# Second norm of the feed-forward blocks: its steps written tile by tile into one slot, between the steps of the tile before the last, with the samples' operands staged

## The chip, the cores and the metric

The kernel runs on one core of a Trainium2 chip. Five engines work from queues of their own: PE (matmuls and transposes, results into PSUM), ACT (activations, copies, square roots), DVE (elementwise work), POOL (elementwise work on SBUF), and SP, which issues DMAs. Each engine works its queue off in the order of the program. The metric is the device time of one execution in microseconds (us). A time is the median of several runs; one further execution carries the hardware profiler.

## The reference

One layer of a decoder runs on a prompt of 2048 rows and on 8 samples of 4 rows (32 rows), with the same weights; the width is 1024. What the change touches is the end of the layer:

```python
y = concat(attention_heads, sgu_heads) @ w_out      # 1024 x 1024
x = x + y                                           # residual
z = rmsnorm(x, g2)                                  # the second norm: x / sqrt(mean(x*x) + 1e-6) * g2
h = silu(z @ w_gate) * (z @ w_up)                   # hidden width 2816
x = x + h @ w_down
out = rmsnorm(x, g_final)
```

## The kernel before

**Blocks.** The prompt is 16 row tiles of 128 rows. The attention comes first; then the out projection and the feed-forward part run in three blocks, `blocks = [Block(0,6), Block(6,12), Block(12,16)]`: block 0 and block 1 have six tiles, block 2 has four and also the 32 sample rows, which it works as a fifth, short tile (number 4 of that block, taken first: the order there is 4, 0, 1, 2, 3). A block goes through these stages:

1. The open units: columns 0 to 511 of the out projection of each tile (`open_part`), added to the residual (`open_end`).
2. The second phase, called so below: columns 512 to 1023 of each tile (`out_part`, L1360 to L1372), which is 24 matmuls with 512 columns for a tile (8 slices, three matmuls each, since a number is kept as a high and a low part), in two halves of 12. Then comes `out_end` (L1374 to L1382, DVE), which adds them to the residual `acc`, and the second norm.
3. The product of the gate and up weights by the normed rows, made from seven products (q0 to q6) in place of eight, over f = 0 to 21 (slices of the hidden width); for f = 0 in two units: unit 1 does the first four tiles (the first two in block 2), unit 2 the other two. Later f do all tiles at once. Between them stand the down products (L1654).

**The second norm of a tile** (L1400 to L1465) goes as follows. `norm2_a`: ACT squares a row and sums it (L1404, or L1411 where no half was squared early). `rms_b`: DVE L1386 and L1387, then ACT's square root (L1388). `norm2_b`: four short steps on DVE (`newton`, L142 to L146), then ACT writes the scaled row into a `pair` tile (L1420). `norm2_c`: eight transposes on PE into the two PSUM banks `ps_t` (L1433), then the operands of the seven products. ACT copies a quarter (L1449) and writes the first high part (L1450), DVE makes sums and differences (L1451, L1453, L1456, L1457) and low parts (L1452, L1458), `split_sb` (L132 to L138) writes the high part of a sum on ACT (L135) and its low part on POOL (L138), ACT writes two high parts from PSUM (L1455). Only when L1458 has read the second bank of `ps_t` may the next tile's transposes go into it. There are two such banks in all. High and low parts go into `xh2` and `xl2` (`B.X`).

**The samples** have four times fewer columns to spread: each of their seven operands is written by `split_sb(at_(hi), at_(lo_), x, eng_lo=dve)` (L1465) into columns 64 to 71 of every tile's place: 7 instructions on ACT and 7 on DVE behind one copy and four sums, from `norm2_c(B, n - 1, B.xns)` at the end of `next_block`, that is after the last tile's `out_part`.

**What sets the order.** Each engine's order is that in which the program is written, and `later(n, fn, ..., ahead=...)` and `tick()` (L1271 to L1282) write it: a `tick` stands ahead of every half of an `out_part`, ahead of every product q, and ahead of every down unit; `later(n, fn)` puts `fn` at the n-th tick from now, and with `ahead=True` in front of the others of that tick. `first_operands` (L1784) lays the weights' operands for f = 0 over ticks 1 to 9 of the second phase: `high` (ACT, L1520) and `low_half` (POOL or DVE, L1524). `next_block` lays `half1_split` (the split of `w_out`'s second half, L135 on ACT and L138 on POOL) at ticks 8, 11, 14 and 17. In before, `norm2_c` of a tile falls between the two halves of a later tile's `out_part`.

**Products.** `product` (L1571) does 12 matmuls into one of four banks `ps_m` and evicts them (L1590 to L1616): q0 on ACT, q1, q3 and q4 on DVE, q2 and q5 with a silu on ACT. The bank of q3 stays in use until the second eviction of q4 (L1602, `c22 = c21 + s1`).

Of the kernel before, what the change touches and what calls it, by code (L numbers as in the profile page):

```python
# [10 lines left out]
F32 = mybir.dt.float32  # L11
# [54 lines left out]
def hymba_step(ctx: ExitStack, tc: tile.TileContext, A: dict, O: dict):  # L66
# [99 lines left out]
    def zn_tile():  # L166
        return rp.tile([P, 512], F32, name="zn", tag="zn", bufs=3)
# [1089 lines left out]
    def square_tile():  # L1257
        return pair_tile(F32).rearrange("p a b -> p (a b)")
# [25 lines left out]
    class Block:  # L1284
        def __init__(self, b0, b1):
            self.b0, self.nt = b0, b1 - b0
            self.last = b1 == NT
            self.rows = [P] * self.nt + ([SR] if self.last else [])

            self.w = 64 + (SR // 2 // self.nt if self.last else 0)  # L1290
            self.acc, self.wo, self.cat, self.late, self.h, self.open, self.s1 = {}, {}, {}, {}, {}, {}, {}

        def place(self):
            self.X = []
# [95 lines left out]
    def rms_c(s1, n):  # L1390
        v, r = s1[:n, 1:2], s1[:n, 2:3]
        newton(r, v)
        return r
# [6 lines left out]
    def norm2_a(B, i, put_off):  # L1400
        n = B.rows[i]
        if i in B.s1:
            s1 = B.s1.pop(i)
            act.activation(B.X[0][:, i, 0:512], B.acc[i][:, 512:1024], AF.Square, accum_out=s1[:, 3:4])  # L1404
            later(1, rms_b, s1, n, s1[:, 3:4])
        else:
            s1 = fl.tile([P, 4], F32, name="s1", tag="s1", bufs=6)

            if n != P:
                B.xns = fc.tile([P, D], F32, name="xns", tag="acc5")  # L1410
            act.activation(B.X[0][:, i, 0:D] if n == P else B.xns[:n], B.acc[i][:n], AF.Square, accum_out=s1[:n, 0:1])  # L1411
            later(1, rms_b, s1, n)

        later(2, norm2_b, B, i, s1, put_off, ahead=True)

    def norm2_b(B, i, s1, put_off):
        n = B.rows[i]
        r = rms_c(s1, n)
        xn = square_tile() if n == P else B.xns
        act.activation(xn[:n], B.acc[i][:n], AF.Copy, scale=r)  # L1420
        if n == P:
            later(2 + put_off, norm2_c, B, i, xn)

    def norm2_c(B, i, xn):

        n = B.rows[i]
        hi, lo_ = B.ops
        pts = []
        for kk in range(2):
            pt = ps_t()  # L1430
            for k in range(4):
                c0 = (kk * 4 + k) * P
                pe.transpose(pt[:, k * P:k * P + n], xn[:n, c0:c0 + P], ident[:n, :n])  # L1433
            pts.append(pt.rearrange("p (k t) -> p k t", k=4)[:, :, 0:n].rearrange("p k (z t) -> p z k t", z=2))
        (b11, b12), (b21, b22) = ((p_[:, 0], p_[:, 1]) for p_ in pts)
        sums = [zn_tile()[:, 0:2 * 4 * (n // 2)].rearrange("p (j k t) -> p j k t", j=2, k=4) for _ in range(2)]
        (t1, t2), (t3, t4) = ((s_[:, 0], s_[:, 1]) for s_ in sums)

        def sums_of():

            act.activation(t4, b12, AF.Copy)
            dve.tensor_sub(t1, t4, b11)
            dve.tensor_sub(t3, b22, t4)
            dve.tensor_sub(t2, b22, t1)
            dve.tensor_sub(t4, b21, t2)

        if n == P:
            at_ = lambda x, j0, j1: x[:, i, j0:j1, :, 0:64]
            act.activation(t4, b12, AF.Copy)  # L1449
            act.activation(at_(hi, 0, 1)[:, 0], b11, AF.Copy)  # L1450
            dve.tensor_sub(t1, t4, b11)  # L1451
            dve.tensor_sub(at_(lo_, 0, 1)[:, 0], b11, at_(hi, 0, 1)[:, 0].bitcast(F32))  # L1452
            dve.tensor_sub(t2, b22, t1)  # L1453
            split_sb(at_(hi, 3, 5), at_(lo_, 3, 5), sums[0])
            act.activation(at_(hi, 1, 3), pts[1], AF.Copy)  # L1455
            dve.tensor_sub(t3, b22, t4)  # L1456
            dve.tensor_sub(t4, b21, t2)  # L1457
            dve.tensor_sub(at_(lo_, 1, 3), pts[1], at_(hi, 1, 3).bitcast(F32))  # L1458
            split_sb(at_(hi, 5, 7), at_(lo_, 5, 7), sums[1])
        else:  # L1460
            sums_of()
            for j, x in enumerate((b11, b21, b22, t1, t2, t3, t4)):
                at_ = lambda y: y[:, :, j, :, 64:].rearrange("p i k c -> p k i c")
                x = x.rearrange("p k (i c) -> p k i c", i=B.nt)
                split_sb(at_(hi), at_(lo_), x, eng_lo=dve)  # L1465

# [262 lines left out]
    def open_end(B, i):  # L1729
        out_end(B, i, 0, B.open.pop(i))  # L1730
# [64 lines left out]
            tick()  # L1795
            open_part(B, i, range(c * 4, c * 4 + 4), c == 0, c == 1)

    def second_unit(B, i):
        ps = ps_o()
        for c in range(2):  # L1800
            tick()
            out_part(B, i, 1, range(c * 4, c * 4 + 4), ps, c == 0, c == 1)
        return ps

    def second_end(B, i, ps, put_off=0):
        out_end(B, i, 1, ps)
        norm2_a(B, i, put_off)

    def first_block(B):

        m1, m2 = acc_place(2), acc_place(4)
        load_cat(B, 1, 0, KD, m1)
        merge_load(h, 2)
        merge_load(h, 3)
        load_cat(B, 2, 0, KD, m2)
        B.place()
        load_cat(B, 3, 0, KD)
        load_cat(B, 0, KD - 1, KD)
        load_acc(B, 1)
# [21 lines left out]
        for i in range(6):  # L1841
            ps = second_unit(B, i)
            if i in (1, 2):
                load_acc(B, 2 * i)
                load_acc(B, 2 * i + 1)
            if i > 1:
                open_end(B, i)
            second_end(B, i, ps, i == 5)

    def first_end(B, i):  # L1850
        open_end(B, i)
# [3 lines left out]
    def next_block(B, downs, finals):  # L1855

        n = len(B.rows)
        order = [n - 1] * B.last + list(range(B.nt))
        B.banks = {i: y for y, i in enumerate(order)}
        B.place()  # L1860
        tiles = [i for i in order if B.rows[i] == P]
        skip = n - len(tiles)
        for j, i in enumerate(tiles):
            if j < 3:
                load_cat(B, i, 0, KD)
            else:
                later(2 * j - 5, load_cat, B, i, 0, KD)
            later(3 + 2 * (j + skip), split_cat, B, i)
        half1_load(*range(4))
        later(3, half1_load, *range(4, KD))  # L1870
        for s in (6, 7):
            later(s - 5, split_wo, B, 0, s, lambda s: op_tile())
        for y, fn in enumerate(finals):
            later(2 + 2 * y, fn)
        for y, i in enumerate(order):
            later(12 + 2 * y, first_end, B, i)
        for y in range(4):
            later(8 + 3 * y, half1_split, B, 2 * y, 2 * y + 1)
            later(10 + 3 * y, sources, B, 0, *((2 * y, 2 * y + 1) if y < 3 else (6,)))
        for fn in downs:  # L1880
            fn()
        for i in order:
            open_unit(B, i)
        first_operands(B)
        for i in order:
            second_end(B, i, second_unit(B, i), i == order[-1])
        if B.last:
            norm2_c(B, n - 1, B.xns)

    for bi, B in enumerate(blocks):  # L1890
        if bi == 0:
# [190 lines left out]
```

## Time and profile before

| | us |
|---|---|
| runs (3) | 2655.63, 2662.3, 2672.53 |
| median | 2662.3 |
| profiled execution | 2665.7 |
| its span | 2663.9 |

The profiled execution lies 3.4 us above the median and within the spread of the runs. All numbers from the trace belong to it. A row of the timeline reads: start in us from the span's start, duration in us, engine, line, operation, output<-inputs, shapes, and how many records it stands for; a bracket at the end gives the idle time of that engine before it and what released it. Durations of matmuls overlap; what a matmul costs is the distance from its start to the next one's. A row of the windows view gives a stretch, its length, PE's busy time with the number of its matmuls, the clock that PE was granted (1.00 is full), the share of DMA and GB/s. A row of a groups view gives the count, the busy time and the mean ns of one, then the engine's idle time ahead of the group and what ended it.

The second phases and unit 1 after them stand in these places: block 0 from 995.97 to 1063.92, block 1 from 1616.80 to 1678.56, block 2 from 2207.24 to 2260.36, where unit 2 starts.

### The profile page before, as it was taken

The page shows a single profiled execution, that of the slowest core. Times are in us where ns is not written, and L with a number is a line of the kernel's source. Part 1 is how long each engine was busy: PE and PEld are TensorE (multiplying, and loading weights), DVE is VectorE, ACT ScalarE, POOL GpSimd, SP SyncE. Part 2 cuts the span into 40 slices and gives each one's busy share as a digit, 9 for nine tenths or more (in the row PEclk, how much of TensorE's full clock was granted, in tenths as well). Part 3 has the DMA queues.
Part 4 walks back from the last instruction along what each step waited for, and adds up shares of the span by engine and source line. Part 5 has one row for each costly group of instructions (what it writes and reads, how often), then busy time and mean ns, then how long its engine had stood idle before and what let it go on. Part 6 is the DMA issues. An engine that isn't in the chain of part 4 may idle for free. (4 is left out here: it accounts for less than half of the span.)

```text
span 2663.9 us, 38923 instructions
## 1 busy us (share of the span) xinstructions
PE 2509.5 (94%) x13587; PEld 2217.7 (83%) x13587; DVE 1419.8 (53%) x2828; ACT 1224.6 (46%) x2570; POOL 1367.8 (51%) x1040
## 2 busy tenths in 40 slices
PE   7999899998999888999999999999999998999997
PEld 6777687677888766898999987899999987999996
DVE  3358785435888845434444464444444465344445
ACT  5414344445887735554454544432333335433333
POOL 1035653132666654776776743554454533666663
PEclk9999999998999998999999999999999999899998
DMA  7765844587688573455463664455463643555553
GB/s 241 220 204 161 277 141 137 171 260 223 186 239 239 138 215 108 147 186 166 161 195 124 194 182 138 165 173 181 150 206 127 221 153 100 186 203 197 198 201 114
DMA packets 313811, 481.06 MB, mean 181 GB/s; under 512 B 25843, under 2 KB 178852, under 8 KB 307728
## 3 DMA queue, kind: packets, MB, share of 16 engines
q1 hardware_dynamic: 301052, 455.89, 53.3%
q10 hardware_dynamic: 12564, 22.68, 3.4%
q8 instruction: 108, 1.77, 0.3%
q14 instruction: 87, 0.71, 0.1%
HBM read 382.76 MB, written 165.84 MB: 206 GB/s over the span
## 5 line engine op out<-in xcount | busy, mean ns | idle before, releaser
L1524 POOL TENSOR_TENSOR op<-fr,op 128x512 fp32r<-128x512 f32 x385 | 488.9, 1297 | 311.1 <-ACT op L1520 291.3
L1581 PE MATMUL ps_m<-xh,op 128*128 128x384 f32 (+4 forms) x1932 | 623.6, 323 | 6.7 <-DVE zn L1602 3.3
L1583 PE MATMUL ps_m<-xh,op 128*128 128x384 f32 (+4 forms) x1932 | 622.0, 322 | 1.7 <-POOL op L1524 1.7
L1582 PE MATMUL ps_m<-xl,op 128*128 128x384 f32 (+4 forms) x1932 | 622.1, 322 | 0.9 <-DVE xl L1452 0.9
L1654 PE MATMUL ps_o<-dw,hw 128*128 128x512 f32 x2040 | 485.9, 393 | 11.8 <-DVE acc L1656 11.8
L1654 PEld LDWEIGHTS ps_o<-dw,hw 128*128 128x128 f32 x2040 | 380.5, 188 | 95.1 <-DVE acc L1656 18.9
L1581 PEld LDWEIGHTS ps_m<-xh,op 128*128 128x128 f32 x1932 | 371.8, 192 | 11.9 <-ACT xh L135 3.7
L1582 PEld LDWEIGHTS ps_m<-xl,op 128*128 128x128 f32 x1932 | 372.2, 193 | 5.4 <-DVE xl L1452 1.3
L1583 PEld LDWEIGHTS ps_m<-xh,op 128*128 128x128 f32 x1932 | 371.7, 192 | 2.1 <-POOL op L1524 2.1
L1656 DVE TENSOR_TENSOR acc<-acc,ps_o 128x512 f32<-128x512 f32 (+1 forms) x362 | 247.0, 687 | 215.0 <-PE ps_o L1654 215.0
L1621 ACT ACTIVATE ps_t<-zn 128x384 f32<-128x384 f32 (+1 forms) x126 | 58.3, 462 | 479.6 <-DVE zn L1604 372.2
L1520 ACT ACTIVATE op<-fr 128x512 fp32r<-128x512 f32 x396 | 235.5, 622 | 24.2 <-DMA fr<-ab_d 14.0
L138 POOL TENSOR_TENSOR dw<-fd,dw 128x1024 fp32r<-128x1024 f32 x66 | 158.7, 2404 | 123.5 <-ACT dw L135 123.1
L318 PE MATMUL ps_s<-wh,xh 128*128 128x512 f32 x480 | 196.8, 410 | 6.5 <-ACT xh L135 6.5
L319 PE MATMUL ps_s<-wl,xh 128*128 128x512 f32 x480 | 191.7, 399 | 4.6 <-DVE wl L226 4.4
L320 PE MATMUL ps_s<-wh,xl 128*128 128x512 f32 x480 | 191.3, 398 | 0.0
L1524 POOL TENSOR_TENSOR op<-pair,op 128x512 fp32r<-128x512 f32 x63 | 81.5, 1301 | 119.1 <-ACT op L1520 119.1
L1631 ACT ACTIVATE hw<-ps_t 128x384 fp32r<-128x384 f32 (+1 forms) x126 | 56.1, 453 | 176.6 <-DVE ps_t L1627 175.7
L318 PEld LDWEIGHTS ps_s<-wh,xh 128*128 128x128 f32 x480 | 92.4, 192 | 35.9 <-issue 8.2
L319 PEld LDWEIGHTS ps_s<-wl,xh 128*128 128x128 f32 x480 | 92.6, 193 | 23.5 <-DVE wl L226 6.3
L320 PEld LDWEIGHTS ps_s<-wh,xl 128*128 128x128 f32 x480 | 92.2, 192 | 20.7 <-POOL xl L138 0.4
L611 POOL TENSOR_TENSOR vl<-kv,vh 100x512 fp32r<-100x512 f32 (+1 forms) x32 | 46.0, 1440 | 109.9 <-ACT vh L605 35.5
(470 smaller groups left out, 4816.7 us busy)
## 6 DMA issues: line engine op xcount, KB each, us to landing
fr<-ab_d SPq DMA_DIRECT2D x308, 256.0 KB
fd<-in_w_down_dram SPq DMA_DIRECT2D x66, 512.0 KB
out_ks_dram<-in_cache_k_dram SPq DMA_DIRECT2D x56, 512.0 KB
out_vs_dram<-in_cache_v_dram SPq DMA_DIRECT2D x56, 512.0 KB
ab_d<-fr SPq DMA_DIRECT2D x88, 256.0 KB
raw<-in_w_in_dram SPq DMA_DIRECT2D x72, 256.0 KB
qk_d<-pair SPq DMA_DIRECT2D x64, 256.0 KB
ab_d<-pair SPq DMA_DIRECT2D x63, 256.0 KB
```

The lines of the kernel that those rows point to most:

```text
L138: (eng_lo or pool).tensor_sub(lo, src, hi.bitcast(F32))
L318: pe.matmul(o[j], xh[:, k, :], wh, start=(k == 0), stop=False)
L319: pe.matmul(o[j], xh[:, k, :], wl, start=False, stop=False)
L320: pe.matmul(o[j], xl[:, k, :], wh, start=False, stop=(k == KD - 1))
L1520: act.activation(ops[f, j][0], ab[f][j], AF.Copy)
L1524: (pool if f or j in POOL_LOW else dve).tensor_sub(lo_, ab[f][j], hi.bitcast(F32))
L1581: pe.matmul(out, wh[:, ks], xh[:, :, k], start=(k == 0), stop=False)
L1582: pe.matmul(out, wh[:, ks], xl[:, :, k], start=False, stop=False)
L1583: pe.matmul(out, wl[:, ks], xh[:, :, k], start=False, stop=(k == 3))
L1621: act.activation(g, c, AF.Silu)
L1654: pe.matmul(ps[0:nr], l_, r_[:, cs], start=(z == 0 and y == 0), stop=(z == FC - 1 and y == len(pairs) - 1))
L1656: dve.tensor_add(B.acc[i][0:nr, cs], B.acc[i][0:nr, cs], ps[0:nr])
```

## The change

The steps of the second norm are no longer put off one by one with `later`, but are written in one function, `norm2_slot(B, k, order)`, which stands ahead of the `out_part` of the k-th tile. It does the second norm's sum, root and scale for the tile whose `out_part` has just ended (`order[k-1]`), woven with the transposes and operands of the tile before that (`order[k-2]`). Two more slots follow the last tile: one ahead of product q0 of unit 1, one ahead of q4 (`later(1, ...)` and `later(5, ...)`, `ahead=True`).

- **Norm.** The instructions of `norm2_a` to `norm2_c` are the same; only their order is new. The operands are in four steps: `first` (PE's transposes, ACT's copy and first high part, DVE's five differences in a row), `second` (a split on ACT and POOL, ACT's two high parts from PSUM), `third` (the other split) and `last` (DVE's low part from PSUM). Between them stand the square, the short steps and the scale of the other tile.
- **Samples.** The short tile's operands are written like any other tile's, into a staged tile `xst` in SBUF, and `place_staged` copies them into columns 64 and on of every tile's place with one instruction on ACT and one on DVE, ahead of the slot that follows the last `out_part` (k = n). With the sums, the samples' operands took 8 instructions on ACT and 11 on DVE; now they take 6 on ACT and 7 on DVE, the two copies among them, and 2 on POOL.
- **Splits of `w_out`.** In block 2 `half1_split` moves from ticks 8, 11, 14, 17 to 8, 10, 12, 14.
- The loads of `acc` of tiles 2 to 5 in block 0 stay at the same place (`more_acc`).

No matmul, transpose or DMA is added or removed.

```diff
+    def norm2_scale(B, i, r):
+        ...
+        act.activation(B.xn[i][:n], B.acc[i][:n], AF.Copy, scale=r)
...
+    class Operands:
+        def __init__(self, B, i):
+            ...
+                    pe.transpose(pt[:, k * P:k * P + n], xn[:n, c0:c0 + P], ident[:n, :n])
+            ...
+            if n == P:
+                self.to = [x[:, i, :, :, 0:64] for x in B.ops]
+            else:
+                t_ = fc.tile([P, D], F32R, name="xst", tag="acc5")
+                B.staged = [t_[:, z * 512:z * 512 + 28 * SR // 2] for z in range(2)]
+                self.to = [x.rearrange("p (j k c) -> p j k c", j=7, k=4) for x in B.staged]
+        def first(self):
+            ...
+            act.activation(t4, b12, AF.Copy)
+            act.activation(hi[:, 0], b11, AF.Copy)
+            dve.tensor_sub(t1, t4, b11)
+            dve.tensor_sub(lo_[:, 0], b11, hi[:, 0].bitcast(F32))
+            dve.tensor_sub(t2, b22, t1)
+            dve.tensor_sub(t3, b22, t4)
+            dve.tensor_sub(t4, b21, t2)
+        def second(self):
+            split_sb(hi[:, 3:5], lo_[:, 3:5], self.sums[0])
+            act.activation(hi[:, 1:3], self.pts[1], AF.Copy)
+        def third(self):
+            split_sb(hi[:, 5:7], lo_[:, 5:7], self.sums[1])
+        def last(self):
+            dve.tensor_sub(lo_[:, 1:3], self.pts[1], hi[:, 1:3].bitcast(F32))
+    def place_staged(B):
+        for z, eng in enumerate((act, dve)):
+            src = B.staged[z].rearrange("p (m i c) -> p i m c", m=28, i=B.nt)
+            dst = B.X[z].rearrange("p i (m w) -> p i m w", m=28)[:, :, :, 64:]
+            ...
+    def norm2_slot(B, k, order):
+        n = len(order)
+        cur = order[k - 1] if 1 <= k <= n else None
+        x = None
+        if k == n and B.last:
+            place_staged(B)
+        if cur is not None:
+            if cur in B.open:
+                open_end(B, cur)
+            out_end(B, cur, 1, B.half1.pop(cur))
+        if 2 <= k:
+            x = Operands(B, order[k - 2])
+            x.first()
+        if cur is not None:
+            s1, more = norm2_square(B, cur, zn_tile() if k == n and B.last else None)
+        if x:
+            x.second()
+        if cur is not None:
+            rms_b(s1, B.rows[cur], more)
+            r = rms_c(s1, B.rows[cur])
+        if x:
+            x.third()
+        if cur is not None:
+            norm2_scale(B, cur, r)
+        if x:
+            x.last()
...
+    def second_phase(B, order, after=None):
+        for k, i in enumerate(order):
+            norm2_slot(B, k, order)
+            B.half1[i] = ps = ps_o()
+            for c in range(2):
+                tick()
+                out_part(B, i, 1, range(c * 4, c * 4 + 4), ps, c == 0, c == 1)
+            if after:
+                after(i)
+        later(1, norm2_slot, B, len(order), order, ahead=True)
+        later(5, norm2_slot, B, len(order) + 1, order, ahead=True)
...
-            later(8 + 3 * y, half1_split, B, 2 * y, 2 * y + 1)
+            later(8 + (2 if B.last else 3) * y, half1_split, B, 2 * y, 2 * y + 1)
...
-        for i in order:
-            second_end(B, i, second_unit(B, i), i == order[-1])
-        if B.last:
-            norm2_c(B, n - 1, B.xns)
+        second_phase(B, order)
```

ACT in block 1, before, one tile's round in the second phase: the square, root and scale of tile 3 stand together, then the operands of the tile whose transposes went into `ps_t0` and `ps_t1` (`zn` are the sums, `xh2` the high parts, `pair` the scaled row):

```order
L1404 ACTIVATE xh2_15487,s1_15916<-acc3_15793 128x512
L1388 ACTIVATE s1_15916<-s1_15916 128x1
L1420 ACTIVATE pair_16182<-acc3_15793,s1_15916 128x1024
L1449 ACTIVATE zn_16195<-ps_t0_16184 128x256
L1450 ACTIVATE xh2_15487<-ps_t0_16184 128x256
L135 ACTIVATE xh2_15487<-zn_16194 128x512
L1455 ACTIVATE xh2_15487<-ps_t1_16189 128x512
L135 ACTIVATE xh2_15487<-zn_16195 128x512
```

The same round of ACT now:

```order
L1444 ACTIVATE zn_16172<-ps_t0_16161 128x256
L1445 ACTIVATE xh2_15487<-ps_t0_16161 128x256
L1406 ACTIVATE xh2_15487,s1_15916<-acc3_15793 128x512
L135 ACTIVATE xh2_15487<-zn_16171 128x512
L1455 ACTIVATE xh2_15487<-ps_t1_16166 128x512
L1389 ACTIVATE s1_15916<-s1_15916 128x1
L135 ACTIVATE xh2_15487<-zn_16172 128x512
L1418 ACTIVATE pair_16193<-acc3_15793,s1_15916 128x1024
```

The same eight instructions stand in another order: the square, the root and the scale of tile 3 are now spread among the operands of the tile ahead of it, and the scaled row comes last.

DVE in the same round, before, from tile 3's `out_end` on:

```order
L1377 TENSOR_TENSOR acc3_15793<-acc3_15793,ps_o3_16095 128x512
L1386 TENSOR_SCALAR s1_15916<-s1_15916 128x1
L1387 TENSOR_SCALAR s1_15916<-s1_15916 128x1
L142 RECIPROCAL s1_15916<-s1_15916 128x1
L144 TENSOR_SCALAR s1_15916<-s1_15916 128x1
L145 TENSOR_SCALAR s1_15916<-s1_15916 128x1
L146 TENSOR_SCALAR s1_15916<-s1_15916 128x1
L1451 TENSOR_TENSOR zn_16194<-zn_16195,ps_t0_16184 128x256
L1452 TENSOR_TENSOR xl2_15488<-ps_t0_16184,xh2_15487 128x256
L1453 TENSOR_TENSOR zn_16194<-ps_t1_16189,zn_16194 128x256
L1456 TENSOR_TENSOR zn_16195<-ps_t1_16189,zn_16195 128x256
L1457 TENSOR_TENSOR zn_16195<-ps_t1_16189,zn_16194 128x256
```

And now:

```order
L1378 TENSOR_TENSOR acc3_15793<-acc3_15793,ps_o3_16129 128x512
L1446 TENSOR_TENSOR zn_16171<-zn_16172,ps_t0_16161 128x256
L1447 TENSOR_TENSOR xl2_15488<-ps_t0_16161,xh2_15487 128x256
L1448 TENSOR_TENSOR zn_16171<-ps_t1_16166,zn_16171 128x256
L1449 TENSOR_TENSOR zn_16172<-ps_t1_16166,zn_16172 128x256
L1450 TENSOR_TENSOR zn_16172<-ps_t1_16166,zn_16171 128x256
L1387 TENSOR_SCALAR s1_15916<-s1_15916 128x1
L1388 TENSOR_SCALAR s1_15916<-s1_15916 128x1
L142 RECIPROCAL s1_15916<-s1_15916 128x1
L144 TENSOR_SCALAR s1_15916<-s1_15916 128x1
L145 TENSOR_SCALAR s1_15916<-s1_15916 128x1
L146 TENSOR_SCALAR s1_15916<-s1_15916 128x1
```

The five differences of the other tile moved ahead of the short steps on `s1`, into the time in which ACT squares tile 3.

PE at the end of block 2's second phase, before: the last slice of the last `out_part`, the samples' transposes (`xns`), and q0 of unit 1 (rows left out in between):

```order
L1367 MATMUL ps_o2_21416<-wol_21211,xh2_20825 128x512
L1368 MATMUL ps_o2_21416<-wol_21211,xl2_20826 128x512
L1433 MATMUL ps_t0_21477<-ident_76,xns_21250 128x32 x4
L1433 MATMUL ps_t1_21482<-ident_76,xns_21250 128x32 x4
L1581 MATMUL ps_m3_21512<-xh2_20825,op_21216 128x136
L1582 MATMUL ps_m3_21512<-xl2_20826,op_21216 128x136
L1583 MATMUL ps_m3_21512<-xh2_20825,op_21216 128x136
```

And now:

```order
L1368 MATMUL ps_o2_21476<-wol_21157,xh2_20825 128x512
L1369 MATMUL ps_o2_21476<-wol_21157,xl2_20826 128x512
L1430 MATMUL ps_t0_21505<-ident_76,pair_21473 128x128 x4
L1430 MATMUL ps_t1_21510<-ident_76,pair_21473 128x128 x4
L1617 MATMUL ps_m3_21541<-xh2_20825,op_21216 128x136
L1618 MATMUL ps_m3_21541<-xl2_20826,op_21216 128x136
L1619 MATMUL ps_m3_21541<-xh2_20825,op_21216 128x136
```

In the samples' place stand the transposes of the last tile but one, which stood inside unit 1 before; the samples' own now stand ahead of tile 1's `out_part`.

More of the change, by code (lines that the diff above doesn't have):

```diff
@@ L1398, in norm2_half, with norm2_square @@
         act.activation(zn_tile(), B.acc[i][:, 0:512], AF.Square, accum_out=s1[:, 0:1])
-    def norm2_a(B, i, put_off):
+    def norm2_square(B, i, junk):
         n = B.rows[i]
[L1402 to L1414, printed above, removed]
@@ L1416, in norm2_b @@
-    def norm2_b(B, i, s1, put_off):
+        s1 = B.s1.get(i)
+        if s1 is not None:
+            act.activation(B.X[0][:, i, 0:512] if junk is None else junk, B.acc[i][:, 512:1024], AF.Square, accum_out=s1[:, 3:4])
+            return s1, s1[:, 3:4]
+        s1 = fl.tile([P, 4], F32, name="s1", tag="s1", bufs=6)
+        if n != P:
+            B.xn[i] = fc.tile([P, D], F32, name="xns", tag="acc5")
+        act.activation(B.X[0][:, i, 0:D] if n == P else B.xn[i][:n], B.acc[i][:n], AF.Square, accum_out=s1[:n, 0:1])
@@ L1417, in norm2_b @@
+        return s1, None
+    def norm2_scale(B, i, r):
         n = B.rows[i]
-        r = rms_c(s1, n)
-        xn = square_tile() if n == P else B.xns
-        act.activation(xn[:n], B.acc[i][:n], AF.Copy, scale=r)
         if n == P:
[L1422 to L1439, printed above, removed]
+            B.xn[i] = square_tile()
+        act.activation(B.xn[i][:n], B.acc[i][:n], AF.Copy, scale=r)
@@ L1456, in norm2_c @@
             dve.tensor_sub(t3, b22, t4)
             dve.tensor_sub(t4, b21, t2)
[L1458 to L1465, printed above, removed]
+        def second(self):
+            hi, lo_ = self.to
+            split_sb(hi[:, 3:5], lo_[:, 3:5], self.sums[0])
+            act.activation(hi[:, 1:3], self.pts[1], AF.Copy)
@@ L1796, in open_unit @@
             open_part(B, i, range(c * 4, c * 4 + 4), c == 0, c == 1)
[L1798 to L1807, printed above, removed]
+    def second_phase(B, order, after=None):
[9 more added lines that the diff above has]
+        later(5, norm2_slot, B, len(order) + 1, order, ahead=True)
     def first_block(B):
@@ L1839, in first_block, with more_acc @@
         first_operands(B)
-        for i in range(6):
-            ps = second_unit(B, i)
+        def more_acc(i):
             if i in (1, 2):
@@ L1845, in first_block @@
                 load_acc(B, 2 * i + 1)
-            if i > 1:
-                open_end(B, i)
-            second_end(B, i, ps, i == 5)
+        second_phase(B, range(6), more_acc)
     def first_end(B, i):
```

30 lines of the change are left out of this document (19 added, 11 removed).

## The prediction

> **What bounds the kernel now.** I read the page first, then the windows of PE over the three second phases, then the view of what PE waits for, then the timelines of PE, ACT and DVE there.
>
> ```profile
> span 2663.9 us, 38923 instructions
> PE 2509.5 (94%) x13587; PEld 2217.7 (83%) x13587; DVE 1419.8 (53%) x2828; ACT 1224.6 (46%) x2570; POOL 1367.8 (51%) x1040
> ```
>
> PE is busy for 94% of the span, no other engine for much over half. So a change that removes no matmul can win only where PE waits or where its clock is down. The change touches three stretches, each from the start of a second phase to the start of unit 2 of f = 0; the fourth row is what follows the third.
>
> ```profile
> 995.97:1063.92 67.95, 55.34 (x277) 0.90 0.36 115
> 1616.80:1678.56 61.76, 52.56 (x277) 0.94 0.25 82
> 2207.24:2260.36 53.12, 43.31 (x237) 0.93 0.29 88
> 2260.36:2283.18 22.82, 22.82 (x105) 0.50 0.35 116
> ```
>
> PE idles 12.6, 9.2 and 9.8 us in them (length less busy time), its clock is under 1.00, and block 2's unit 2 runs wholly at half clock. What PE waits for:
>
> ```profile
> PE ps_t L1433 <- DVE xl L1458: 16.3, 9, 2.6
> PE ps_t L1433 <- DVE xl L1452: 5.5, 4, 2.0
> PE ps_m L1581 <- DVE zn L1602: 3.3, 3, 2.1
> PE ps_o L1372 <- POOL wol L138: 1.6, 2, 1.0
> ```
>
> The first two rows are the transposes, which wait until DVE has read the previous tile's two banks; the third is unit 2's first product, which waits for the bank of q3; the fourth is the split of w_out in block 2.
>
> What the work itself costs PE at full clock is in these starts:
>
> ```profile
> 2222.22 0.39 PE L1366 MATMUL ps_o<-woh,xh 128*128 128x512 f32 x1
> 2227.78 1.03 PE L1433 MATMUL ps_t<-ident,pair 128*128 128x128 f32 x8
> 2228.57 0.47 PE L1366 MATMUL ps_o<-woh,xh 128*128 128x512 f32 x1
> ...
> 1660.06 0.28 PE L1583 MATMUL ps_m<-xh,op 128*128 128x256 f32 x1
> 1660.42 0.28 PE L1583 MATMUL ps_m<-xh,op 128*128 128x256 f32 x1
> ...
> 2252.10 0.28 PE L1581 MATMUL ps_m<-xh,op 128*128 128x136 f32 x1
> 2252.43 0.28 PE L1581 MATMUL ps_m<-xh,op 128*128 128x136 f32 x1
> ...
> 2266.16 0.41 PE L1581 MATMUL ps_m<-xh,op 128*128 128x136 f32 x1
> 2266.80 0.41 PE L1581 MATMUL ps_m<-xh,op 128*128 128x136 f32 x1
> ```
>
> The 24 matmuls of a tile take 5.56, its eight transposes 0.79: 6.35 us a tile. A product matmul takes 0.12 with 256 columns and 0.11 with 136 (three in 0.36 and in 0.33), or 0.213 at half clock (three in 0.64). Blocks 0 and 1 then need 6 x 6.35 + 84 x 0.12 = 48.2 us, block 2 4 x 6.35 + 16 x 0.23 + 0.3 for the samples + 84 x 0.112 = 38.8. Lost are 67.95 - 48.2 = 19.75, 61.76 - 48.2 = 13.6 and 53.12 - 38.8 = 14.3 us, and in the half-clock stretch 22.82 x (1 - 0.112/0.213) = 10.8: 58.5 in all. More than that this change can't bring.
>
> **The chain that makes PE wait.** One tile's round in block 1:
>
> ```profile
> 1645.73 0.63 PE L1433 MATMUL ps_t<-ident,pair 128*128 128x128 f32 x4 [2.02 <-DVE xl L1458]
> ...
> 1646.21 0.63 ACT L1404 ACTIVATE xh<-acc 128x512 fp32r<-128x512 f32 x1 [0.56 <-DVE acc L1377]
> 1647.41 0.20 ACT L1388 ACTIVATE s<-s 128x1 f32<-128x1 f32 x1 [0.47 <-DVE s L1387]
> 1648.65 1.15 ACT L1420 ACTIVATE pair<-acc,s 128x1024 f32<-128x1024 f32 x1 [1.04 <-DVE s L146]
> 1654.82 0.63 ACT L1404 ACTIVATE xh<-acc 128x512 fp32r<-128x512 f32 x1 [0.56 <-DVE acc L1377]
> ...
> L135 ACT ACTIVATE xh<-zn 128x512 fp32r<-128x512 f32 x8 | 5.0, 630 | 8.6 <-DVE zn L1453 4.8 <-DVE zn L1457 3.8
> L1455 ACT ACTIVATE xh<-ps_t 128x512 fp32r<-128x512 f32 x4 | 2.3, 580 | 0.0
> L1449 ACT ACTIVATE zn<-ps_t 128x256 f32<-128x256 f32 x4 | 1.5, 364 | 0.0
> ...
> L1458 DVE TENSOR_TENSOR xl<-ps_t,xh 128x512 fp32r<-128x512 f32 x4 | 2.7, 680 | 0.0
> L1456 DVE TENSOR_TENSOR zn<-ps_t,zn 128x256 f32<-128x256 f32 x4 | 1.7, 425 | 4.7 <-ACT xh L1455 4.7
> ```
>
> Square to square is 8.61 us, against 6.35 that PE needs. ACT and DVE hand to each other in turn: ACT waits 0.56, 0.47, 1.04, and twice over 0.95 for a sum.
>
> **The change, part by part.**
>
> *The weaving.* The instructions are the same, so busy times stay; what goes is the waiting in turn. From the end of a tile's last matmul the new round runs: out_end and the first transposes, 0.7 (out_end adds 512 columns on DVE, as L1458's 0.68); ACT's copy 0.36; DVE's five differences at 0.42, 2.1, while ACT squares; the short steps and root, 0.47 + 0.20 + 1.04; the scale 1.15. That is 6.0, with the hand-over to PE about 6.2: just under PE's 6.35, which hides it. ACT's own work in a round, 0.36 for the copy, as much for a high part of that size, 0.73 for the square (from 1646.21 to 0.47 before 1647.41), 2 x 0.63, 0.58, 0.20 and 1.15, is 4.6 and fits too. A weight's high part (0.62, two in a round) that falls in between makes it about 6.45, so 0.1 waits a round, 0.2 over a block where the cover is thin. DVE's last step (0.68, reading the second bank) ends before the scale does, so the banks are no longer the last to arrive; the scaled row is.
>
> *Block 0* has four high parts and DVE lows between two of its slots:
>
> ```profile
> 1019.48 1.78 DVE L1524 TENSOR_TENSOR op<-fr,op 128x512 fp32r<-128x512 f32 x1
> ...
> L1524 DVE TENSOR_TENSOR op<-fr,op 128x512 fp32r<-128x512 f32 x1 | 0.7, 680 | 0.0
> L1520 ACT ACTIVATE op<-fr 128x512 fp32r<-128x512 f32 x1 | 0.6, 617 | 0.0
> ```
>
> A low part takes 0.68 alone and took 1.78 beside POOL. Two high parts more on ACT give a wait of 1.2, one low part 0.8 to 1.7 (I take 1.25), and 0.2 for the rest: 2.65.
>
> [...]
>
> *The end of the second phase.* The last tile's slot stands ahead of q4, and unit 2's first product takes the bank that q4's second eviction frees on DVE, behind that slot's differences. ACT does q0's eviction, a table load and a silu ahead of that slot:
>
> ```profile
> 1671.46 1.28 ACT L1621 ACT_TABLE_LOAD   x1
> ```
>
> From the start of the slot ahead of q0 the row of work is: that slot's round, 6.0; two activations of 256 columns at 0.36 and the load, 2.0; the last slot's copy, five differences and low part, 0.36 + 2.1 + 0.68; q4's two evictions at 0.42. That is 12.0, and with hand-overs of 0.1 each about 12.8, against PE's 84 x 0.12 + 2 x 0.79 = 11.7: a wait of 1.1. In block 2 PE's products are shorter (9.4 + 1.6 = 11.0) and two samples' copies come ahead: about 1.4. Bounds: 0.6 and 2.1, from the third row of PE's waits (three waits, 3.3 in all, the longest 2.1, so about 0.6 for each of the others).
>
> *Samples and splits in block 2.* The earlier splits of w_out take away waits of PE's sample part (1.6 us in two waits by the view above, longest 1.0). The splits now stand one to three ticks earlier on ACT and POOL, among the open units, where both have room (ACT and POOL are near half busy). No DMA is moved. The samples' first transposes may wait for the scaled row, up to 0.9; I take 0.9. place_staged is one copy of 448 elements on each of ACT and DVE; between 0.36 (256, L1449) and 0.68 (512, L1458), taken 0.6, beside PE's last matmuls. Fourteen short splits after the end are gone.
>
> *Sum.* Left over are 2.65 + 1.1 = 3.75 in block 0, 0.2 + 1.1 = 1.3 in block 1, 0.9 + 1.4 = 2.3 in block 2. Gains: 16.0 + 12.3 + 12.0 = 40.3. If unit 2 of block 2 also runs at full clock, 10.8 more: 51.1. Against the profiled 2665.7 (3.4 above the median of 2662.3, which I don't take off, but let into the range) that gives 2625.4 or 2614.6.
>
> **Which of the two.** The clock falls behind waits:
>
> ```profile
> 1654.33 0.63 PE L1433 MATMUL ps_t<-ident,pair 128*128 128x128 f32 x4 [2.04 <-DVE xl L1458]
> 2260.36 0.45 PE L1581 MATMUL ps_m<-xh,op 128*128 128x136 f32 x1 [2.09 <-DVE zn L1602]
> ...
> 1645.00:1650.00 5.00, 4.27 (x21) 1.00 0.00 0
> 1655.00:1660.00 5.00, 4.57 (x14) 0.66 0.00 0
> ```
>
> Behind 2.02 (1645.73) it stayed at 1.00; behind 2.04 it was 0.66; behind 2.09 it was 0.50 for 22.82 us. A single wait of 1.4 behind a full stretch is below all of these, so I take full clock.
>
> **The rivals.**
>
> A, as reckoned, with full clock in unit 2: 2614.6. Chance 0.46.
>
> B, the same, but the last wait in block 2 is near 2 and the half clock stays: 2625.4. For it: the wait depends on a chain of ACT, DVE and PE whose hand-overs I estimate. Chance 0.24.
>
> C, the change doesn't do what it says: the round stays near 8 us, since ACT and DVE still hand over in turn and POOL slows DVE (1.78 for 0.68). 14 rounds x (8.0 - 6.35) = 23 us are given back: 2614.6 + 23 = 2638, within 1%. Against it: ACT's own 4.6 in a round of 8.61. Chance 0.12.
>
> R, the waits aren't what lowers the clock. Then only idle time comes back: 12.6 + 9.2 + 9.8 - 7.35 = 24.2, so 2641.5. For it speaks the window at 1.00 behind 2.02; against it the half clock begins exactly at the longest wait of block 2's unit. Chance 0.07. [...]
>
> D, slower: the round gets as long as before's 8.61 and each tile's 24 matmuls follow a wait of over 2 us, so that they run at 0.66 each time. That gives back 14 x 2.26 = 31.6, costs 14 x 5.56 x (1/0.66 - 1) = 40 more, and 10.8 for unit 2: 2614.6 + 82.4 = 2697. It decides from a round of about 8.3 us (a wait of 2). Before, only some rounds waited so long, which is why its clock was 0.90 to 0.94. Chance 0.07; other ways 0.04, half of them slower.
>
> **How the numbers follow.** A is likeliest: 2615. All left-over waits gone as well (7.35) and the 3.4 of the median give 2604 as the low end. The upper end takes in B, C and R: 2642. D stays out. One per cent, about what a measurement of this kernel can tell from no change, is 26.6 us, so faster means under 2635.7. A and B lie there, with a third of C: 0.74. Within 1% are the rest of C, R and a part of the others: 0.16. Slower are D, half of what is left and a little of C: 0.10.
>
> **What would show it.** In the profile after, the two rows of PE's transposes waiting should fall from 21.8 us to under 5, and what ends their waits should be ACT's scaled row, not DVE's low part. Squares in blocks 1 and 2 should be 6.3 to 6.5 us apart; 8 means C or D. The stretches from the second phase to unit 2 should take about 52, 49.5 and 41 us. Unit 2 of block 2 should take about 12 us, or 23 under B. The waits at L1372 should be gone. I am wrong if the short steps on DVE stand behind a slow low part in most rounds, or if a wait near 2 us comes back at the end of a second phase.

## The result and the profile after

| | before | after |
|---|---|---|
| median, us | 2658.97 (4 runs) | 2628.48 (4 runs) |
| profiled execution, us | 2665.7 | 2627.61 |
| its span | 2663.9 | 2625.8 |

The ratio is 0.9876, with a 95% interval of 0.9844 to 0.9908: the changed kernel is 30.5 us (1.2%) faster by the medians and 38.1 by the two profiled spans. The page of the changed kernel, and its windows of PE cut at the same places as before (second phase of block 0, 1 and 2 are the second, fourth and sixth row; the others lie between):

```profile
span 2625.8 us, 38945 instructions
PE 2501.6 (95%) x13587; PEld 2212.1 (84%) x13587; DVE 1420.9 (54%) x2824; ACT 1224.1 (47%) x2568; POOL 1369.1 (52%) x1042
```

```profile
0.00:987.41 987.41, 904.18 (x4800) 0.96 0.69 205
987.41:1039.89 52.48, 48.85 (x277) 1.00 0.46 150
1039.89:1590.94 551.05, 539.50 (x2785) 1.00 0.53 171
1590.94:1640.98 50.04, 48.48 (x277) 1.00 0.30 101
1640.98:2177.67 536.69, 535.65 (x2753) 0.98 0.52 173
2177.67:2224.83 47.16, 43.33 (x237) 0.93 0.32 106
```

Two of the same rows of the kernel before, for the stretches that the prediction did not cut out:

```profile
0.00:995.97 995.97, 904.29 (x4799) 0.96 0.68 203
1678.56:2207.24 528.68, 527.69 (x2753) 1.00 0.53 177
```

| mark | before | after | earlier by |
|---|---|---|---|
| block 0, start of the second phase | 995.97 | 987.41 | 8.6 |
| its unit 2 | 1063.92 | 1039.89 | 24.0 |
| block 1, start of the second phase | 1616.80 | 1590.94 | 25.9 |
| its unit 2 | 1678.56 | 1640.98 | 37.6 |
| block 2, start of the second phase | 2207.24 | 2177.67 | 29.6 |
| its unit 2 | 2260.36 | 2224.83 | 35.5 |
| end of the span | 2663.9 | 2625.8 | 38.1 |

The first 8.6 us lie ahead of all changed work. Over the eleven kernels of this study that first mark lies anywhere from 981.6 to 996.0 in the profiled executions, so it is spread, not gain. From that mark to the end the kernel before takes 1667.9 us and the changed one 1638.4: the change is worth 29.5 us there, which agrees with the medians. I use this time, called "from the mark" below, to compare profiles.

The stretches show a gain in all three second phases (15.5, 11.7 and 6.0 us), and a loss of 8.0 between the second phase of block 1 and that of block 2, where no instruction was moved: PE idles 1.0 us there in both kernels, but its clock is 0.98 in place of 1.00. What PE waits for now:

```profile
PE ps_m L1617 <- DVE zn L1638: 3.9, 3, 1.4
PE ps_t L1430 <- ACT pair L1418: 2.6, 4, 1.3
PE ps_o L1373 <- POOL wol L138: 1.6, 1, 1.6
PE ps_o L1372 <- ACT wol L135: 0.7, 1, 0.7
```

The transposes' waits fell from 21.8 us to 2.6, and what ends them is ACT's scaled row, no longer DVE's low part. The squares of block 1 on ACT:

```profile
1597.32 0.63 ACT L1406 ACTIVATE xh<-acc 128x512 fp32r<-128x512 f32 x1 [0.18 <-DVE acc L1378]
...
1629.06 0.63 ACT L1406 ACTIVATE xh<-acc 128x512 fp32r<-128x512 f32 x1
```

These are the first and the last of six, so a round takes 31.74 / 5 = 6.35 us, just what PE needs for a tile. The loss is in these rows, PE in the first 20 us after unit 2 of block 1 starts, and the row of PE at its start:

```profile
1640.00:1650.00 10.00, 9.02 (x54) 0.68 0.32 104
1650.00:1660.00 10.00, 10.00 (x43) 0.50 0.61 212
...
1039.89 0.30 PE L1617 MATMUL ps_m<-xh,op 128*128 128x128 f32 x1 [1.29 <-DVE zn L1638]
1640.98 0.30 PE L1617 MATMUL ps_m<-xh,op 128*128 128x128 f32 x1 [1.29 <-DVE zn L1638]
2224.83 0.30 PE L1617 MATMUL ps_m<-xh,op 128*128 128x136 f32 x1 [1.36 <-DVE zn L1638]
```

Unit 2 waits 1.3 us in each block, for the bank of q3. In block 0 nothing follows. In blocks 1 and 2 the clock falls to half some 2.5 us after the wait and stays there for 17 us each time.

### The profile page after: what moved, and what is told of

The parts are those of the page before. It is cut to its first block, busy times and chain, and to the rows that moved or that the text cites. A ratio compares the mean times of both kernels' runs of the same rounds, so it can differ in the third digit from the quotient of the medians.

```text
span 2625.8 us, 38945 instructions
## 1 busy us (share of the span) xinstructions
PE 2501.6 (95%) x13587; PEld 2212.1 (84%) x13587; DVE 1420.9 (54%) x2824; ACT 1224.1 (47%) x2568; POOL 1369.1 (52%) x1042
## 5 line engine op out<-in xcount | busy, mean ns | idle before, releaser
L1690 PE MATMUL ps_o<-dw,hw 128*128 128x512 f32 x2040 | 484.9, 392 | 12.8 <-DVE acc L1692 11.6
```

The costliest lines, as they stand in the source:

```text
L1690: pe.matmul(ps[0:nr], l_, r_[:, cs], start=(z == 0 and y == 0), stop=(z == FC - 1 and y == len(pairs) - 1))
```

## The experiments

Theory N was: the half clock comes where a wait and a stretch of little streaming on PE fall together, and the products with 128 or 136 columns don't easily bring it back. Rival W was: a wait alone decides, or the narrow products fall to half clock whatever the wait. All experiments start from the changed kernel unless said otherwise.

**Banks for unit 2.** The first two products of unit 2 take the two banks of the out projection, which lie idle then:

```diff
-        ps = ps_m()[:, 0:n]
+        ps = (ps_o() if u["n"] == 1 and q < 2 else ps_m())[:, 0:n]
```

> Theory N: the half clock in unit 2 comes from a stretch with little streaming on PE (a wait of 1.3 us, the transposes ahead of it, then matmuls of 128 or 136 columns, which take 0.11 us where 512 columns take 0.23) and stays until wide matmuls come. With the two idle out-projection banks for unit 2's first two products the wait of 1.29 to 1.36 us ahead of unit 2 falls to 0.4 or less, the clock stays full there, and the half-clock stretches in blocks 1 and 2 (about 8 and 10 us lost) go: about 2628 - 3 - 18 = 2607. Rival W (narrow products alone fall to half clock by chance, whatever the wait): only the waits go, about 2625.

Measured: 2614.44 us, ratio to the kernel before 0.9836 (0.9792 to 0.988); from the mark 1619.2, which is 19.2 less than the changed kernel. The three second phases and the first half of unit 2 in block 2:

```profile
993.88:1044.98 51.10, 48.76 (x277) 1.00 0.47 155
1597.88:1646.71 48.83, 48.56 (x277) 1.00 0.31 103
2175.34:2220.00 44.66, 41.88 (x237) 0.96 0.34 113
2220.00:2231.50 11.50, 11.50 (x103) 1.00 0.44 154
```

The wait ahead of unit 2 is gone and so is each half-clock stretch behind it (1.00 in the last row). Block 1 to block 2 takes 2175.34 - 1646.71 = 528.6, as in the kernel before. So the 8 us lost there, and what unit 2 of block 2 lost, hang on that wait of 1.3 us. This speaks against narrow products falling by themselves.

**Three tiles and three.** Unit 1 and unit 2 of blocks 0 and 1 take 192 columns each:

```diff
-        part = 4 if B.nt == 6 else 2
+        part = 3 if B.nt == 6 else 2
```

> Units of f = 0 in blocks 0 and 1 take three and three tiles (192 columns) in place of four and two (256 and 128). Theory N: 192 columns stream more of the time, so unit 2 of block 1 doesn't stay at half clock even after the same wait of 1.3 us: 8 us less, about 2620; block 2 is unchanged, its half clock stays. Rival W (the wait alone decides): the half clock comes and stays for all of unit 2, about 2628 to 2632.

Measured: 2624.18 us, ratio 0.9879 (0.9842 to 0.9917); from the mark 1633.3. The waits are 1.54, 1.54 and 1.36. In block 1:

```profile
1641.49 0.37 PE L1617 MATMUL ps_m<-xh,op 128*128 128x192 f32 x1 [1.54 <-DVE zn L1638]
...
1640.00:1650.00 10.00, 8.51 (x62) 0.83 0.24 79
```

The clock falls here too, at once, but it is back after 3.4 us (1641.64 to 1645.05; the 0.83 of the row says the same), where 128 columns kept it down for 17. In block 2, with 136 columns as before, it stays at half for 20 us. So wider products ended the half clock here; they didn't prevent it. Rival W, by which it stays for all of unit 2, is out.

**Wide filler.** Twelve matmuls of 512 columns, whose result nobody reads, stand ahead of q2 of unit 2:

```diff
+        if u["n"] == 1 and q == 2:
+            wide = ps_o()
+            for k in range(12):
+                pe.matmul(wide, ops[f, q][0][:, 0:P], ops[f, q][0], start=(k == 0), stop=(k == 11))
```

> The changed kernel with twelve matmuls of 512 columns, whose result nobody reads, ahead of q2 of unit 2 in each block (2.7 us at full clock each). Theory N: the wide matmuls bring the clock back to full at half-clock stretches, so of unit 2 in blocks 1 and 2 only some 4 to 6 us run at half clock in place of 13 to 17. Rival W: the clock stays at half until unit 2 ends, and the filler takes 5.5 us there. The time: 2628 + 3 x 2.7 - 10 = 2626 under N, 2628 + 14 = 2642 under W.

Measured: 2622.43 us in one run; from the mark 1635.0. The clock falls in all three blocks now, block 0 among them, and each time comes back with the filler:

```profile
1040.00:1050.00 10.00, 10.00 (x65) 0.83 0.21 79
1640.00:1650.00 10.00, 8.72 (x51) 0.83 0.24 79
2220.00:2230.00 10.00, 8.65 (x38) 0.66 0.26 79
```

By these rows it lasts 3.4, 3.4 and 6.8 us (a row of 10 us at 0.83 has 3.4 us at half). That is as theory N has it: the filler ended the half clock, and with 36 more matmuls the kernel was no slower in this one run.

**The kernel before with the two banks alone.** The edit is that of the first experiment.

> The kernel before with the two banks alone. Theory: the wait of 2.09 us ahead of unit 2 of block 2 was the same bank, and the half-clock stretch of 22.8 us behind it cost 10.8; both go, as do two waits of 0.6: 2659 - 14 = 2645. Rival: in the kernel before, the last tile's operands are late anyway, the wait and the half clock stay: 2659.

Measured: 2649.09 us, ratio 0.9965 (0.9949 to 0.9981); from the mark 1659.7, 8.2 less than the kernel before. The wait of 2.09 and the half clock behind it are gone, but block 2 has another one earlier. The clock falls at 2233.93, within the second of two waits of the samples' transposes (1.57 and 2.59 us), ahead of unit 1, whose first product then waits too:

```profile
2234.60 0.60 PE L1433 MATMUL ps_t<-ident,xns 32*128 32x32 f32 x4 [2.59 <-DVE xl L1458]
2236.54 0.48 PE L1581 MATMUL ps_m<-xh,op 128*128 128x136 f32 x1 [1.33 <-ACT xh L135]
...
2230.00:2240.00 10.00, 4.51 (x25) 0.70 0.00 0
2240.00:2250.00 10.00, 10.00 (x49) 0.50 0.00 0
2250.00:2260.00 10.00, 10.00 (x87) 0.95 0.01 2
```

It ends at 2251, after 17 us, while all products still have 136 columns. The kernel before has a half clock behind the same two waits, which is over after 6.8 us (2242.33 to 2249.16). So my "stay at half until wide ones come" is too strong: under products of 136 columns the clock came back after 6.8 and 17 us here, and in block 2 of the changed kernel it didn't in the 13.3 us of them.

**Splits of w_out back at their ticks.**

```diff
-            later(8 + (2 if B.last else 3) * y, half1_split, B, 2 * y, 2 * y + 1)
+            later(8 + 3 * y, half1_split, B, 2 * y, 2 * y + 1)
```

> Only the earlier ticks of the splits of w_out in block 2 are undone (11, 14, 17 again). Theory: the move put the last split on ACT behind the half square of a tile at the same tick, which made PE wait 0.74 + 1.55 us in the samples' part and lowered the clock for some 6 us after it; undone, the waits are 0.56, 0.56 and 0.99 as before the change and the clock stays up: about 3 us less, 2625. Rival, as the prediction had it: the move helps, and undoing it costs 1 to 2 us, 2630.

Measured: 2623.26 us, ratio 0.9891 (0.9843 to 0.994); from the mark 1629.3. The ratio can't be told from the changed kernel's 0.9876 (0.9844 to 0.9908). The second phase of block 2 takes 2220.41 - 2174.39 = 46.0, against 47.16. PE's waits for the splits there are in this experiment:

```profile
PE ps_o L1373 <- POOL wol L138: 1.5, 2, 1.0
...
PE ps_o L1373 <- POOL woh L138: 0.7, 2, 0.6
```

2.2 us, against 1.6 + 0.7 = 2.3 with the move. The move gave nothing. The 1.1 us isn't shown to be its doing either: the half clock behind these waits lasts 6.8 us in the changed kernel and 3.4 here, but it lasts 3.4 as well in the two experiments above that keep the move and the wait, and their second phases of block 2 take 45.6 and 46.1. The rest of what this profile gains from the mark is block 1, whose half clock did not come in this execution (2174.39 - 1645.71 = 528.7) behind the same wait of 1.28.

**Unwoven.** The slots stay, but the square, root and scale stand ahead of the other tile's operands:

```diff
+        if cur is not None:
+            s1, more = norm2_square(B, cur, zn_tile() if k == n and B.last else None)
+            rms_b(s1, B.rows[cur], more)
+            r = rms_c(s1, B.rows[cur])
+            norm2_scale(B, cur, r)
         if 2 <= k:
             x = Operands(B, order[k - 2])
             x.first()
-        ...
+            x.second()
+            x.third()
+            x.last()
```

> The slots stay where they are, but within a slot the square, root and scale of one tile stand ahead of the operands of the other, as before the change. Theory: the weaving itself makes the round short; without it a round is about 8 us again, PE waits about 2 us ahead of each tile's transposes (14 rounds), with some clock loss: about 2628 + 28 to 45 = 2656 to 2673. Rival: the place of the transposes at a tile's start is what helps; then the round stays near 6.5 us and the time at 2628 to 2638.

Measured: 2672.38 us, ratio 1.0063 (1.0041 to 1.0084): slower than the kernel before. Its second phases of blocks 0 and 1, three squares of block 1, and PE's main wait:

```profile
993.13:1062.60 69.47, 55.85 (x277) 0.90 0.34 112
1614.34:1676.22 61.88, 52.20 (x277) 0.94 0.24 81
```

```profile
1626.15 0.63 ACT L1406 ACTIVATE xh<-acc 128x512 fp32r<-128x512 f32 x1 [0.26 <-DVE acc L1378]
1635.88 0.63 ACT L1406 ACTIVATE xh<-acc 128x512 fp32r<-128x512 f32 x1 [1.50 <-DVE acc L1378]
1645.71 0.63 ACT L1406 ACTIVATE xh<-acc 128x512 fp32r<-128x512 f32 x1 [2.00 <-DVE acc L1378]
...
PE ps_t L1430 <- DVE xl L1463: 20.0, 12, 2.1
```

Two rounds of 9.7 and 9.8 us (the others in block 1 take 5.4 to 8.1), and two stretches of about the length they had before the change (67.95 and 61.76). Without the weaving the place at a tile's start gives none of the gain in these stretches; the weaving in the old place was not run. That the time is above the kernel before comes behind them: a half clock of 20 us in unit 2 of block 1 (9.6 us lost) and one in block 2 that lasts at least from 2255.95 to 2280 (three products of 136 columns take 0.64 us there).

**Block 2's opening, three ways.** All three have the two banks. In the first the splits stand at ticks 8, 9, 10 and 11:

```diff
-            later(8 + (2 if B.last else 3) * y, half1_split, B, 2 * y, 2 * y + 1)
+            later(8 + (1 if B.last else 3) * y, half1_split, B, 2 * y, 2 * y + 1)
```

> The banks of the first experiment, and in block 2 the splits of w_out at ticks 8, 9, 10, 11, ahead of all half squares. Theory: the last split stood on ACT behind the half square at its tick; ahead of it PE's waits in the samples' part (2.2 to 2.7 us) and the clock dip behind them (about 2 to 3 us) go: 2614 - 4 to 5 = 2610. Rival: POOL's or the loads' pace sets the splits (they land when they land, or crowd ACT and POOL in the open units): 2614 or more.

Measured: 2615.2 us, ratio 0.9837 (0.9822 to 0.9852); from the mark 1622.5, against 1619.2 with the banks alone. PE's waits for the splits are gone, and in their place stands:

```profile
2186.47 1.06 PE L1430 MATMUL ps_t<-ident,xns 32*128 32x32 f32 x8 [5.15 <-ACT xns L1418]
...
2182.73 1.05 ACT L1411 ACTIVATE xns<-acc 32x1024 f32<-32x1024 f32 x1 [2.44 <-DMA out_yp_dram<-acc]
```

The samples' scaled row is late, and its square names a store: by this row the buffer still holds a finished tile that is on its way to memory. So I put the row into another ring:

```diff
-            B.xn[i] = fc.tile([P, D], F32, name="xns", tag="acc5")
+            B.xn[i] = square_tile()
```

> The banks and the splits at ticks 8 to 11, and the samples' scaled row in the pair ring in place of the buffer whose store to memory it waits for (ACT waits 2.44 us, named by the store). Theory: the store holds the samples' chain by about 1 us only, since DVE's two adds end 1 us before; the wait of 5.15 falls to about 4.1, 2614. Rival: the store is the whole wait, and it falls to under 2.5 with the clock dip gone, 2610.

Measured: 2607.31 us, ratio 0.9809 (0.9758 to 0.9859); from the mark 1622.4, no less than the one before.

```profile
2177.38 1.06 PE L1430 MATMUL ps_t<-ident,pair 32*128 32x32 f32 x8 [4.15 <-ACT pair L1418]
...
2165.99 0.20 ACT L1389 ACTIVATE s<-s 128x1 f32<-128x1 f32 x1 [3.66 <-DVE s L1388]
2171.61 0.57 ACT L1381 ACTIVATE zn<-ps_o 32x512 f32<-32x512 f32 x1
...
2167.36 0.40 PE L1373 MATMUL ps_o<-wol,cats 128*64 128x512 f32 x1
```

The wait falls by 1.0 as expected. The rest is that ACT begins the samples' fold at 2171.61, four us after their last matmul started on PE (2167.36), with no idle time just ahead of it. It works its queue in order, and shortly before it stood idle for 3.66, 0.39 and 2.02 us, each time for DVE, which was still at the last norms of block 1 and the sums of the open units. So ACT was late rather than full. The lower time of the profiled execution lies ahead of the mark (981.6).

In the third, the splits at ticks 8 to 11 and the old ring, with tile 0 ahead of the samples in the second phase:

```diff
         first_operands(B)
+        if B.last:
+            order[0:2] = [order[1], order[0]]
         second_phase(B, order)
```

> The banks and the splits at ticks 8 to 11, and in block 2's second phase the samples come second, behind tile 0. Theory: PE's wait of 5.15 us ahead of the samples' transposes comes from work that ACT and DVE still have from the open units and the final norms of block 1 when the samples' norm should start; tile 0, whose half is squared early, takes their place, and both have a tile's 5.5 us more: the wait falls under 1.5 us and the clock dip behind it goes, 2615 - 5 to 6 = 2609. Rival: the samples are late for their own chain (fold of the two halves, square, root, scale, with the store ahead of it), or tile 0 now waits as long: 2613 to 2617.

Measured: 2608.62 us, ratio 0.9815 (0.9763 to 0.9868); from the mark 1620.4. The samples wait 1.67 instead of 5.15, but the tiles' transposes wait 5.1 us in all (2.6 in the first of these three). The second phase takes 2214.48 - 2169.15 = 45.3, against 47.7 (splits early) and 44.7 (banks alone). None beats the banks alone from the mark, in one profile each.

## Why the prediction was right, and where a term was off

**The weaving: right.** The forecast stretches of blocks 0 and 1 were 52 and 49.5 us; measured 52.48 and 50.04. A round was to be 6.3 to 6.5; it is 6.35, so rivals C and D (the round stays long) are out. The unwoven kernel shows that there is no gain without the weaving.

**The end of the second phase: right.** The wait was put at 1.1, and 1.4 in block 2; it is 1.29, 1.29 and 1.36, at the bank named. For block 2 that is partly luck: the row of work of 12.8 against PE's 11.0 gives 1.8, and the samples' copies come on top; the 1.4 does not follow from these terms.

**The clock: wrong, the largest term.** The step was: "A single wait of 1.4 behind a full stretch is below all of these, so I take full clock." I counted 10.8 us won in block 2 by it and nothing lost in block 1. The runs show a half clock behind waits of 1.27 to 1.54. Take the changed kernel and the three woven experiments that kept the wait, three blocks each: the clock fell in 8 of 12 unit 2s (block 0 in one of four, block 1 in three, block 2 in all four). In the four changed kernels with the banks, where the wait is gone, it fell in none of 12. So the wait is needed here, and its length alone does not decide.

What else does is in the traces. In each of the eleven, the clock changes only at moments that lie whole multiples of 3.41 us apart: the 49 changes in the kernel before and the 45 in the changed kernel within 0.01 us, those that rows of matmuls show in the nine others within 0.2. Where this grid lies against the program differs between executions: unit 2 of block 1 starts 0.8 us behind such a moment in the changed kernel and 0.5 with the splits back at their ticks. Here are such stretches in the changed kernel, each with the next one, at the start of unit 2 in block 0, block 1 and block 2:

```profile
1039.42:1042.84 3.42, 2.94 (x27) 1.00 0.21 75
1042.84:1046.25 3.41, 3.41 (x33) 1.00 0.44 160
1640.17:1643.59 3.42, 2.61 (x24) 1.00 0.00 0
1643.59:1647.00 3.41, 3.41 (x19) 0.50 0.17 15
2223.85:2227.26 3.41, 2.43 (x22) 1.00 0.02 5
2227.26:2230.68 3.42, 3.42 (x18) 0.50 0.34 85
```

The waits of blocks 0 and 1 are equal, but of the first 0.5 us lie in the stretch in which unit 2 starts, and of the second 0.8: that leaves 27 matmuls of 128 columns (3456 columns) against 24 (3072). Counted so, by the columns of the matmuls that start in the emptiest stretch that the wait touches, the 8 places where the clock fell have 2176 to 3072, and the 4 where it didn't have 3328 to 3840. A stretch full of products of 128 columns, without a wait, has 30 or 31 of them (3840 or more). The two waits of 1.63 ahead of unit 2 in the unwoven kernel fit as well (3712, no fall; 2944, fall). So in these places narrow products and a wait add up, and where the wait lies on the grid decides. Once at half clock, a stretch has 16 products: with 192 columns (3072) the clock came back after one stretch, with 136 (2176) mostly not: in block 2 of the changed kernel it didn't in three full ones.

The half clock cost 8.0 in block 1, and of the 10.8 in block 2 only 2.6 came. Rival B had the second of these, not the first. With the banks the time from the mark is 48.7 us below the kernel before, near the 51.1 that I reckoned for full clock, but not term by term: waits of 3.6 us that the forecast left in are gone, and block 2's second phase still gains 3.5 less than forecast.

**Block 2's opening: wrong.** The step was: "The earlier splits of w_out take away waits of PE's sample part", with at most 0.9 for the samples' row. PE's waits for the splits became 2.3 us in place of the 1.6 that were to go, and the clock fell within the second:

```profile
2179.43 0.20 ACT L1389 ACTIVATE s<-s 128x1 f32<-128x1 f32 x1 [3.73 <-DVE s L1388]
...
2181.32 0.44 PE L1372 MATMUL ps_o<-wol,cats 128*64 128x512 f32 x1 [0.74 <-ACT wol L135]
2183.32 0.69 PE L1373 MATMUL ps_o<-wol,cats 128*64 128x512 f32 x1 [1.55 <-POOL wol L138]
...
2183.00:2189.00 6.00, 5.56 (x13) 0.50 0.99 325
```

The stretch took 47.16 us, not 41, and gained 6.0, not 12.0. Of the 6 us missing, PE's idle time is 1.5 (3.8 against the 2.3 left over in the forecast) and the clock of 0.93 up to 3.3; about 1 has no place. I read POOL and ACT as having room since they are half busy over the span. Room in time is not room in the queue: ACT stood idle for 3.73 us there, since the next step in its queue, the root of one of block 1's last norms, waited for DVE; then came one of block 2's half squares, and the last split stands behind both. Moving the splits ahead shows what is late next: the samples' row, by 4.2 to 5.2 us. The prediction put 0.9 there and showed no chain for it.

**Other terms.** Rival R (waits don't lower the clock) is out by the first experiment. The time of 2628.5 lies 13.9 us above the forecast and inside the range, near B's 2625.4, for a reason that B had only in part. As a gain it is further off: 51.1 us were forecast and 29.5 came from the mark on. Block 1's half clock, what unit 2 of block 2 did not win and block 2's opening miss 8.0, 8.2 and 6.0 of it. That the time looks closer is luck of the starting point: the forecast counted down from 2665.7, and the changed kernel was compared with a median of 2658.97.

**Open.** The count of columns separates the places in these traces, but no run moved a wait along the 3.41 us on purpose, and how low the count may go was not measured. The few us of block 2's opening are placed on ACT's and DVE's queues by timeline rows and by what moved when the wait moved; no run took that work away from there.

## What to carry to other kernels

Where two engines hand to each other in turn within one item's chain, interleave two items on both queues and reckon the round against the bound engine's need: here 8.6 us became 6.35 with no instruction removed. After that, look at the waits that are left ahead of narrow matmuls: 1.3 us of wait cost 8.0 us at half clock in block 1, and two idle PSUM banks took both away. When a small wait goes, check what was late behind it: in block 2 the waits of 2.3 us for the splits hid that of 5.15 for the samples' row. And an engine that is half busy can still be late, when it works in order and a step ahead waits for another engine: ACT, busy for 47% of the span, stood idle for 3.73 us ahead of the splits.

## What the runs showed of the hardware

In 8 of 12 places a wait of 1.27 to 1.54 us on PE ahead of matmuls with 128 to 192 columns was followed by half the granted clock within 2.6 us, in the changed kernel for 17 us; I had not expected it under 2 us. The clock changed only on a grid of 3.41 us; in these places it fell behind stretches of at most 3072 columns and not behind those of 3328 or more. In the changed kernel matmuls of 384 or 272 columns ended the half clock after 4.1 and 3.7 us; with products of 192 columns it lasted 3.4, with a filler of 512 it lasted 3.4 (6.8 in block 2). Twice it ended under products of 136 columns: 17 us after it began in the kernel before with the banks, and 6.8 in the kernel before.

The stretch ahead of the mark, whose instructions no experiment changed, took 981.6 to 996.0 us over eleven profiled executions. With it, a difference of some us between two profiled spans says little; times from a mark say more.
